# A two-layer hybrid diffusion step on one core: the queue order taken from another timing model

## The chip, the cores and the metric

The kernel runs on one core of one Trainium2 chip. The metric is device time in microseconds (us). Three runs of the kernel before took 2752.75, 2754.29 and 2756.11 us; their median, 2754.29, is the time before.

## What is computed

One inference step of a backbone with two layers (DEPTH = 2) and model width 1024. There are 128 context tokens and 1024 latent tokens, 1152 in all, everything in float32. Each layer does this:

```
h = rmsnorm(x) * (1 + scale) + shift          # shift, scale, gate from silu(cond) @ ada_w + ada_b
a_in, a_gate, f_in, f_gate, q, k, v, c_gate = split(h @ w_in)
ya = S5 diagonal state space, both directions, then gelu and a GLU with glu_w
yf = real part of a 2-D DFT over positions and channels, @ fnet_w
yc = grouped-query attention (8 heads, 2 kv heads, softmax over 1152 keys for latents)
proj = each of ya*silu(a_gate), yf*silu(f_gate), yc*silu(c_gate) @ w_branch[n]
g = sigmoid(h @ merge_w + merge_b);   x = x + gate * (sum(g * proj) @ w_out)
```

A last RMS norm follows. The outputs are both token sets, the context keys and values, and the context's final S5 states.

## The kernel before

Activations are kept transposed, channels on the 128 partitions and tokens along the free axis, in three tiles of 384 tokens. Every float32 operand of a dense product is split in two parts, a high part in the matmul format fp32r (`hh`, `whi`, made by a copy on ACT) and the remainder (`hl`, `wlo`, made by a subtraction on DVE or, for weights, on POOL). A product is then three matmuls: high by high, low by high, high by low (`mm3`, with the matmul itself in line 168).

A dense block (`dense`) is 128 output columns. For each token tile it runs 4 or 8 times three matmuls into a PSUM tile `pd`, of which there are two; then ACT or DVE evacuates it, mostly into `jo` (three slots), and SP stores `jo` to memory. `dense_ahead` loads weights into `wst` (four slots) up to three units ahead and splits them into `whi` and `wlo` (three slots each) one unit ahead.

Beside the dense blocks run the generators of the branches. `drive` and `run_some` interleave them in the program by fixed weights: the S5 setup and states (`state_gen`), the scan (`scan_gen`, 128 steps of four DVE operations each on the state tile, in the trace called `A` with the scratch tiles `ss_s`), the q, k and v part (`qkv_gen`), the S5 output matrices (`ssm_out_gen`, tiles `ss_CA`, `ss_CK`, `ss_Hg`), its result reloaded from memory (`zload_gen`, from the tensors `ydp` and `ydl`, into `jt` and `jo`), the Fourier branch (`fnet_gen`, tiles beginning `fn_`), and attention (`attn_gen`: scores in `pa`, softmax into `at_P`, transposes in `pt`, products with V in `pv`, with dense blocks between).

The context's final states are copied out by `finals`, which `scan_gen` calls behind its last step, though the column that it reads is complete after step 16:

```python
for k in range(128):
    ...                       # four DVE operations a step
    yield 800
self.finals(l)                # act(fin, H[:, :, :, 16]), transposes, a store
```

All this is only the program's order, and it is not the order in the queues. The whole program is one block of a tile framework. When the block closes, a scheduler plays the instructions through a timing model. Each time an engine can take an instruction in the model, it gets the first one in the program's order whose inputs are there and whose output has a free slot, at the model's time. So an instruction may overtake earlier ones of its engine that are not ready in the model. The sequence found this way is written into the engine's queue (DMA issues into SP's or POOL's), the slots are fixed with it, and semaphore waits are added where data cross engines. On the chip each queue runs strictly in that sequence: if the instruction at its head has to wait, all behind it wait too.

The change and the prediction touch no line of the generators. They speak of `finals` and `scan_gen` (the DVE operations are recorded at line 145, ACT's at line 142, which are helpers), of `dense` and its evacuations, of `zload_gen`, `fnet_gen` and `attn_gen`.

## Time and profile before

| what | value |
|---|---|
| median of three runs | 2754.29 us |
| profiled execution, its own time | 2752.03 us |
| its span, first to last instruction | 2750.3 us |
| mean granted PE clock | 0.985 |
| PE, PE's weight loads | 2627.0 us (96%), 2509.0 us (91%) |
| DVE, ACT, POOL | 1826.6 (66%), 1143.5 (42%), 683.4 us (25%) |
| DMA | 366.85 MB, mean 133 GB/s |

The profile is of one execution. Busy times overlap between engines. A row of the timeline has the start, the duration, the engine, the line, the operation with its output and inputs, and in brackets how long the engine was idle before it and what released it. A wait for several events is put down to the last one by the profile. The granted clock is the share of full speed that TensorE got.

### The profile page before, as it was taken

The numbers are of one execution on the slowest core, as the hardware profiler recorded it, in microseconds if no ns is written. First come the engines' busy times: TensorE is split into PE (matmuls) and PEld (weight loads), VectorE is DVE, ScalarE is ACT, GpSimd is POOL, SyncE is SP. The second block draws the span as 40 slices with busy tenths as digits, with TensorE's granted clock in tenths as the row PEclk, the third lists the DMA queues.
The fourth block names the chain that finished last, engine by engine and source line by source line (L and its number), as shares of the span: only waits on it lengthen the run. The fifth ranks groups of instructions, "written<-read, shape, count | busy, mean of one in ns | idle before, by whom it ended". The sixth has DMA issues, their size and how long they took to land. (4 is left out here: it accounts for less than half of the span.)

```text
span 2750.3 us, 44553 instructions
## 1 busy us (share of the span) xinstructions
PE 2627.0 (96%) x16092; PEld 2509.0 (91%) x16092; DVE 1826.6 (66%) x3933; ACT 1143.5 (42%) x2676; POOL 683.4 (25%) x521
## 2 busy tenths in 40 slices
PE   7998999899999999999999899999999999999998
PEld 3898999799999999999989899989989998999998
DVE  6549955856558889866572797577654788891343
ACT  5461145331355565423345322543223655553244
POOL 3241122322321020132343212233222202102223
PEclk9999999999999999999999999999999999999999
DMA  6632223566263345544543222345645334433244
GB/s 223 178 99 84 95 87 110 150 191 207 86 202 114 110 138 153 173 126 114 165 146 93 95 89 84 107 125 160 211 154 174 109 121 150 143 121 98 80 121 149
DMA packets 459997, 366.85 MB, mean 133 GB/s; under 512 B 72953, under 2 KB 432001, under 8 KB 459777
## 3 DMA queue, kind: packets, MB, share of 16 engines
q1 hardware_dynamic: 458480, 359.75, 42.9%
q0 software_dynamic: 1296, 4.26, 0.5%
q8 instruction: 127, 2.08, 0.3%
q14 instruction: 94, 0.76, 0.1%
HBM read 243.52 MB, written 120.39 MB: 132 GB/s over the span
## 5 line engine op out<-in xcount | busy, mean ns | idle before, releaser
L168 PE MATMUL pd<-hh,whi 128*128 128x384 f32 x2496 | 857.1, 344 | 24.0 <-ACT jo L142 20.1
L168 PE MATMUL pd<-hh,wlo 128*128 128x384 f32 x2496 | 844.6, 339 | 3.2 <-POOL wlo L145 3.2
L168 PE MATMUL pd<-hl,whi 128*128 128x384 f32 x2496 | 843.1, 338 | 1.3 <-DVE hl L149 1.3
L145 POOL TENSOR_TENSOR wlo<-wst,whi 128x512 fp32r<-128x512 f32 x312 | 437.9, 1405 | 1525.8 <-ACT whi L142 1404.8
L168 PEld LDWEIGHTS pd<-hh,whi 128*128 128x128 f32 x2496 | 472.5, 189 | 35.0 <-ACT jo L142 22.8
L168 PEld LDWEIGHTS pd<-hh,wlo 128*128 128x128 f32 x2496 | 472.5, 189 | 7.8 <-POOL wlo L145 5.7
L168 PEld LDWEIGHTS pd<-hl,whi 128*128 128x128 f32 x2496 | 473.1, 190 | 3.8 <-DVE hl L149 2.3
L168 PE MATMUL pd<-A,whi 128*128 128x384 f32 x1728 | 458.2, 342 | 8.2 <-ACT jo L142 4.9
L168 PEld LDWEIGHTS pd<-A,whi 128*128 128x128 f32 x1728 | 311.2, 189 | 11.7 <-ACT jo L142 5.6
L142 ACT ACTIVATE whi<-wst 128x512 fp32r<-128x512 f32 x312 | 196.0, 630 | 278.5 <-PE pd L168 190.6
L168 PE MATMUL pd<-A,wlo 128*128 128x384 f32 x864 | 293.9, 340 | 0.0
L1078 DVE TENSOR_REDUCE at_mx<-pa 128x1 f32<-128x1152 f32 x128 | 173.3, 1354 | 16.1 <-PE pa L168 15.7
L168 PE MATMUL pa<-at_K,at_Q 128*128 128x384 f32 x768 | 167.2, 347 | 8.6 <-ACT at_P L142 5.8
L142 ACT ACTIVATE at_PT<-pt 128x384 fp32r<-128x384 f32 (+1 forms) x260 | 114.9, 490 | 144.0 <-PE pt L173 143.6
L142 ACT ACTIVATE at_P<-pa,at_mx 128x1152 f32<-128x1152 f32 x128 | 158.1, 1235 | 20.7 <-DVE at_mx L1078 19.4
L168 PEld LDWEIGHTS pd<-A,wlo 128*128 128x128 f32 x864 | 163.2, 189 | 0.1
L168 PEld LDWEIGHTS pa<-at_K,at_Q 128*128 128x128 f32 x768 | 128.3, 188 | 29.0 <-ACT at_P L142 25.5
L168 PE MATMUL pt<-qkW,hh 128*128 128x384 f32 x576 | 150.7, 343 | 0.0
L168 PE MATMUL pv<-at_PT,at_V 128*128 128x256 f32 x1152 | 148.8, 283 | 0.0
L168 PEld LDWEIGHTS pv<-at_PT,at_V 128*128 128x128 f32 x1152 | 144.7, 191 | 0.8
L142 ACT ACTIVATE jo<-pd 128x384 f32<-128x384 f32 x120 | 58.0, 485 | 198.1 <-PE pd L168 96.5
L145 DVE TENSOR_TENSOR at_PT<-pt,at_PT 128x384 fp32r<-128x384 f32 (+1 forms) x260 | 133.1, 550 | 10.0 <-ACT at_PT L142 7.8
(294 smaller groups left out, 3772.3 us busy)
## 6 DMA issues: line engine op xcount, KB each, us to landing
aw<-in_ada_w_dram SPq DMA_DIRECT2D x48, 512.0 KB, 4.8
wst<-in_merge_w_dram SPq DMA_DIRECT2D x96, 256.0 KB, 3.0
wst<-in_w_in_dram SPq DMA_DIRECT2D x80, 256.0 KB, 2.9
td<-jo SPq DMA_DIRECT2D x96, 192.0 KB, 2.3
jt<-td SPq DMA_DIRECT2D x96, 192.0 KB, 2.8
wst<-in_w_out_dram SPq DMA_DIRECT2D x64, 256.0 KB, 2.9
sgd<-jo SPq DMA_DIRECT2D x72, 192.0 KB, 2.0
jt<-sgd SPq DMA_DIRECT2D x64, 192.0 KB, 2.7
```

The costliest lines, as they stand in the source:

```text
L142: return self.nc.scalar.activation(out, in_, func, **kw)
L145: return (e or self.nc.vector).tensor_tensor(out=out, in0=a, in1=b, op=op)
L168: return self.nc.tensor.matmul(out, w, x, start=first, stop=last, **kw)
L1078: nc.vector.tensor_reduce(out=mx[:, 0:1], in_=src, axis=AX.XY if m3 else AX.X, op=OP.max, negate=True)
```

## The change

One argument of the tile context is set. It selects the timing model that the scheduler plays the program through: a detailed timeline model (devices, queues and DMAs with states of their own) in place of the default, rougher one. The traced instructions, their engines and their sizes are the same; what the scheduler decides by them, the sequence in each queue, the slots and the waits that follow from these, is decided anew.

```diff
-    with tile.TileContext(nc) as tc, ExitStack() as ctx:
+    with tile.TileContext(nc, schedule_with_timeline_sim=True) as tc, ExitStack() as ctx:
         Program(ctx, tc, I, O).run()
```

## Rows read from the trace of the kernel before

**Rows 1.** The page's busy times: engine, busy us, share of the span, instructions.
```profile
PE 2627.0 (96%) x16092; PEld 2509.0 (91%) x16092; DVE 1826.6 (66%) x3933; ACT 1143.5 (42%) x2676; POOL 683.4 (25%) x521
```

**Rows 2.** Stretches: length, busy us (instructions) of each engine, clock, DMA share, GB/s.
```profile
196.00:430.00 234.00, 222.94 (x1282) 220.65 (x1281) 185.52 (x621) 69.91 (x217) 54.90 (x43) 0.97 0.31 96
482.00:607.00 125.00, 115.43 (x772) 105.96 (x771) 91.13 (x195) 41.98 (x83) 36.69 (x28) 0.97 0.57 161
798.00:1165.00 367.00, 357.48 (x2376) 340.83 (x2376) 305.89 (x515) 200.81 (x413) 57.49 (x48) 1.00 0.44 136
...
1540.00:1772.00 232.00, 220.72 (x1268) 218.10 (x1268) 182.92 (x609) 68.24 (x212) 53.23 (x43) 0.97 0.31 96
...
2140.00:2482.00 342.00, 333.37 (x2234) 317.34 (x2232) 287.82 (x484) 189.54 (x389) 54.00 (x45) 1.00 0.42 130
```

**Rows 3.** PE's waits over the span: for what, us in total, times, longest us.
```profile
PE pd L168 <- ACT jo L142: 25.1, 8, 7.8
...
PE pt L173 <- DVE at_P L1082: 8.4, 13, 1.0
PE pt L168 <- issue: 7.3, 3, 3.4
...
PE pd L168 <- POOL wlo L145: 3.2, 5, 1.5
```

**Rows 4.** Timeline of ACT in the first layer's scan.
```profile
210.78 0.63 ACT L142 ACTIVATE whi<-wst 128x512 fp32r<-128x512 f32 x1 [1.43 <-PE pd L168]
223.66 0.32 ACT L142 ACTIVATE ss_fin<-A 128x64 f32<-128x64 f32 x1 [12.25 <-DVE A L145]
223.89 0.61 ACT L142 ACTIVATE whi<-wst 128x512 fp32r<-128x512 f32 x1
224.41 0.85 ACT L142 ACTIVATE jo<-pd 128x384 f32<-128x384 f32 x2
```

**Rows 5.** Timeline of PE behind its two longest waits for `jo`.
```profile
224.93 0.69 PE L168 MATMUL pd<-hh,whi 128*128 128x384 f32 x1 [7.84 <-ACT jo L142]
...
1566.74 0.69 PE L168 MATMUL pd<-hh,whi 128*128 128x384 f32 x1 [7.83 <-ACT jo L142]
```

**Rows 6.** Stretches behind these waits, columns as in rows 2.
```profile
225.00:229.00 4.00, 4.00 (x13) 4.00 (x14) 3.79 (x14) 0.26 (x1) 0.85 (x1) 0.50 0.50 164
229.00:233.00 4.00, 4.00 (x20) 4.00 (x19) 3.72 (x17) 0.49 (x1) 0.00 (x0) 0.81 0.02 4
233.00:250.00 17.00, 17.00 (x100) 17.00 (x100) 16.11 (x54) 4.27 (x8) 4.70 (x4) 1.00 0.24 80
...
1567.00:1571.00 4.00, 4.00 (x13) 4.00 (x14) 3.79 (x15) 0.07 (x1) 0.67 (x1) 0.50 0.51 164
1571.00:1575.00 4.00, 4.00 (x22) 4.00 (x22) 3.73 (x17) 0.49 (x1) 0.00 (x0) 0.88 0.01 2
```

**Rows 7.** Timeline of DVE in the first layer's scan; the last row ends it.
```profile
200.76 1.25 DVE L145 TENSOR_TENSOR ss_s<-ss_AR,A 128x128 f32<-128x128 f32 x1
...
203.69 0.38 DVE L145 TENSOR_TENSOR ss_s<-ss_s,A 128x128 f32<-128x128 f32 x1
204.10 1.41 DVE L145 TENSOR_TENSOR A<-ss_s,ss_s 128x128 f32<-128x128 f32 x1
...
357.88 0.28 DVE L145 TENSOR_TENSOR A<-ss_s,ss_s 128x64 f32<-128x64 f32 x1
```

**Rows 8.** Timeline of POOL at the same place.
```profile
203.97 1.29 POOL L145 TENSOR_TENSOR wlo<-wst,whi 128x512 fp32r<-128x512 f32 x1 [2.20 <-ACT whi L142]
```

**Rows 9.** Timeline of ACT: two instructions that waited for a DMA.
```profile
614.32 0.52 ACT L142 ACTIVATE A<-jo 128x384 fp32r<-128x384 f32 x1 [4.32 <-DMA jo<-ydl]
...
682.64 0.21 ACT L142 ACTIVATE fn_EO<-fn_X 128x2 f32<-128x2 f32 x1 [8.67 <-DMA thb<-jo]
```

**Rows 10.** Timeline of PE behind them.
```profile
616.63 0.69 PE L168 MATMUL pd<-A,whi 128*128 128x384 f32 x1 [3.01 <-ACT jo L142]
...
683.39 0.44 PE L168 MATMUL pd<-hh,whi 128*128 128x384 f32 x1 [1.71 <-ACT jo L142]
```

## The prediction

> **What bounds the kernel now.** I read the busy times first: PE is busy 96% of the span, DVE 66% [rows 1]. So 2750.3 - 2627.0 = 123.3 us is all that PE stands idle, and nearly all that an order can give back; no instruction is taken away. Then I cut the span into stages [rows 2]. The reader is to see that the two layers give the same table twice, that the attention stages already run PE at 97.4% and 97.5%, and that the stage with the S5 output matrices has only 92.3%. Third, what PE waits for [rows 3]: one pair, a dense block's `pd` waiting for ACT to empty the last one into `jo`, holds 25.1 us in eight waits. Fourth, the timeline around the two longest of the eight.
>
> They are the clearest case of what an order can do. `ss_fin`, the copy of the prompt's final states, is written in the program behind all 128 steps of the scan. In ACT's queue it stands far ahead of that place, because its input is complete after step 16. On the chip ACT reached it at 211.4 and stood until DVE had that step, 12.25 us [rows 4]. Behind it in the same queue lay a weight split `whi` and the two `jo` copies that PE needed, so PE stood 7.84 us; in the second layer it stood 7.83 us in the same way [rows 5]. Nothing that PE needs comes from `ss_fin`.
>
> **The change, part by part.** Instructions, sizes and data flow stay; what moves is the place of each instruction in its engine's queue (SP's issues among them) and, with it, which buffer slot it takes. So every term is a wait that goes or comes.
>
> (a) `ss_fin`. What it costs today is more than the two stalls: after them PE's granted clock was 0.50 and 0.81 in two stretches of 4 us. At the full rate of 100 matmuls in 17 us, 4 us hold 23.5; there were 13 and 20, so 14 are missing, worth 14 x 0.17 = 2.4 us. The second layer had 13 and 22, worth 2.0 us [rows 6]. The price is 7.84 + 2.4 + 7.83 + 2.0 = 20.1 us. The cover is good: ACT was held 12.25 us and PE only 7.84, so 4.4 us of lateness are free, and a place that is too late costs nothing, as only an output copy follows. The term lies between 0 (the same place) and -20.1. I take -15: nearer the full end, because ss_fin need not be placed right, only some 8 us later, and the place of today shows a model in which the scan runs much too fast. What is late next? The scan itself ends at 357.9 [rows 7], while its states are first used in the stage that begins at 482; that PE comes 10 us earlier to the stage behind it leaves over 100 us, so nothing takes the gain back.
>
> [...] A step's last add took 1.41 us, from 204.10, where the operation before it took 0.38; POOL ran a 1.29 us split from 203.97. The one at 200.76 took 1.25 us [rows 7, 8]. [...]
>
> (b) The other six waits for `jo`, 25.1 - 15.7 = 9.4 us. Two are shown: ACT's queue is headed by an instruction that waits for a DMA, 4.32 us for a reload of `ydl` and 8.67 us at the input of the Fourier stage [rows 9], and PE waits behind it 3.01 and 1.71 us [rows 10]. The second layer has the like. A place behind `jo` would free them, and how late those loads land is what a rough price misses. Between 0 and -9.4 I take half, -4.7, since the loads are needed soon after and cannot move far.
>
> (c) Waits that the new order brings. No row shows them. They could be nil (no new wait). The nearest rows for the other end are those PE waits that come from a splitter or evacuation just too late: 3.2 us in 5 for `wlo`, 8.4 us in 13 for the scaled softmax [rows 3]. I take +4.7, nearer the lower of the two; the large end is the first rival. SP's order belongs here: a weight load that is issued a unit later shows as one more wait for `wlo`, 1.5 us at the longest [rows 3].
>
> (d) Start and end are left as they are: the first inputs and the last stores follow from data, not from order.
>
> The sum is -15 - 4.7 + 4.7 = -15 us. The profiled execution took 2752.0 us (its span 2750.3 and 1.7 around it), 2.3 under the median 2754.3. So 2752.0 - 15 + 2.3 = 2739 us on the scale of the median.
>
> **The rivals.**
>
> First, slower: attention loses its cover. In these stages PE mixes dense blocks of 12 matmuls between scores, transposes and PV, so that dense work fills the time a softmax takes on DVE and ACT. The greedy choice takes any ready matmul; a model in which PE's own queue fills ahead, or softmax lands later, hands out the dense blocks before the softmax needs cover, and PE then waits at the transposes. For it: DVE is 83% busy there (305.89 of 367), and each of the 128 passes hangs on it. Against it: only two `pd` buffers exist, so no more than two blocks can run ahead. Price: today the two stages idle 9.5 + 8.6 = 18.1 of 709 us; at the 7.7% of the S5 output stage they would idle 54, so +36 [rows 2]. With -15 from (a) that is 2752.0 + 36 - 15 + 2.3 = 2775 us; with no gain, 2790. It decides the sign from the point where attention idles over 15 us more, or 33 against 18.
>
> Second, slower: a new block at a queue's head of the size of `ss_fin`, one in each layer, while `ss_fin` stays or takes another bad place. Many instructions stand early in ACT's and DVE's queues on the strength of a modelled time (table copies, next-layer loads), and any could be the next. The price is that of rows 4 to 6, +20.1, less the 9.4 of (b) at best: between 2765 and 2774 us. Against it: the two layers are alike, so it takes only one wrong price, but a finer model has fewer of them.
>
> Third, no difference: the new model shares the old one's price of the scan, `ss_fin` stays, and the small waits change places. Then the time is that of today within a few us, 2749 to 2760. For it: nearly all of PE's order follows from the program's own order and the few buffers, which stay. That the option does nothing at all is part of this.
>
> **How the numbers follow.** The forecast has 0.47, the first rival 0.27, the second 0.11, no difference 0.15. What a measurement of this kernel can tell from no change is about 0.2%, 5.5 us, so faster is 0.47, same 0.15, slower 0.38. The chances lie close because the gain rests on one kind of wait, seen and priced, while the loss needs no more than a slightly wrong order where PE has least to spare. The forecast's own range runs from 2709 to 2749: its lower end is -20.1 - 9.4, less the 7.3 us of PE's waits at an issue and the 8.4 behind the softmax, -45.2 [rows 3]. The first rival without any gain ends at 2790, so the range for the time is 2709 to 2791; a total loss of attention's cover, or every middle wait gone at once, is left outside.
>
> **What would show it.** Right: `ss_fin` stands behind several more `jo` copies in ACT's order, ACT no longer waits 12 us for it, the two 7.8 us stalls and the clock of 0.50 behind them are gone, and PE's waits for `jo` fall from 25 to some 5 us. (b) right: ACT's waits for `ydl` and for the Fourier input no longer have a `jo` directly behind them. (c) right: PE's idle time in the attention stages stays near 18 us. Wrong: these stages idle over 33 us, PE waits at transposes for the softmax's scale, or ACT has a new single wait over 8 us with a `jo` behind it; and if both 7.8 us stalls are there unchanged, the step that failed is (a).

## The result, and the profile after

The changed kernel takes 2936.55 us in the median (four runs, 2931.53 to 2940.29). The kernel before, with a fourth run beside the three on which the forecast rests, takes 2753.64. The ratio is 1.0662 [1.0642, 1.0681] (the brackets hold the 95% interval): the changed kernel is slower. The forecast was 2739, the range ended at 2791, and of its rivals the first, attention losing its cover, had the right sign and place. The profiled execution took 2931.53 us with a span of 2929.7, which is 179.4 us more than before.

The busy times of the changed kernel, to be read against [rows 1]:

```profile
PE 2672.2 (91%) x16092; PEld 2551.4 (87%) x16092; DVE 1820.2 (62%) x3933; ACT 1153.9 (39%) x2676; POOL 673.5 (23%) x521
```

Each engine has the instructions that it had. PE now stands idle 2929.7 - 2672.2 = 257.5 us where it stood 123.3, and it is busy 45.2 us longer with the same 16092 matmuls; the mean granted clock is 0.969 after 0.985. So 134 us are waits. Most of the other 45 lie where the clock was lower. The clock records of the two traces hold two values, 1.0 and 0.5, and PE was busy 58.3 us at 0.5 before and 138.5 us after. Dense matmuls in a row began 0.32 us apart at 0.5 and 0.173 apart at 1.0 (the medians, the same in both traces), so 80.2 us more at 0.5 cost an estimated 80.2 x (1 - 0.173 / 0.32) = 37.

Next, where. Both spans are cut at the same landmarks, the first score matmul and the last PV product of each attention; columns as in rows 2. The kernel before:

```profile
0.00:768.10 768.10, 714.88 (x4205) 663.45 (x4206) 497.09 (x1286) 295.25 (x783) 213.84 (x165) 0.97 0.46 140
768.10:1145.00 376.90, 367.30 (x2444) 349.64 (x2443) 311.06 (x524) 203.99 (x429) 57.94 (x48) 1.00 0.44 136
1145.00:2106.20 961.20, 920.17 (x5501) 892.25 (x5500) 615.63 (x1448) 343.26 (x867) 281.32 (x204) 0.98 0.44 133
2106.20:2482.20 376.00, 367.21 (x2443) 349.82 (x2442) 311.01 (x524) 204.13 (x429) 57.86 (x48) 1.00 0.44 135
2482.20:2750.30 268.10, 257.39 (x1507) 253.88 (x1505) 91.79 (x151) 96.91 (x172) 72.43 (x56) 0.99 0.36 110
```

The same five stretches after:

```profile
0.00:809.50 809.50, 731.78 (x4252) 676.87 (x4253) 492.72 (x1289) 293.64 (x784) 214.19 (x166) 0.96 0.43 132
809.50:1247.30 437.80, 378.28 (x2418) 359.59 (x2416) 310.52 (x527) 214.69 (x433) 57.03 (x47) 0.96 0.39 123
1247.30:2226.40 979.10, 926.72 (x5526) 899.56 (x5527) 615.99 (x1445) 336.79 (x862) 273.17 (x205) 0.98 0.43 128
2226.40:2663.80 437.40, 381.38 (x2417) 362.80 (x2415) 310.95 (x527) 214.69 (x432) 57.04 (x47) 0.96 0.39 123
2663.80:2929.70 265.90, 254.01 (x1484) 252.53 (x1483) 90.06 (x145) 94.13 (x166) 72.12 (x56) 0.98 0.35 105
```

The two attention stages have 60.9 and 61.4 of the 179.4 us, the stretch ahead of the first attention 41.4, the one between the two 17.9, the end -2.2. Attention holds 26 matmuls fewer in each layer than before, so the time is not for more work: idle time rose from 9.6 + 8.8 to 59.5 + 56.0 us (97 us), busy time by 11.0 + 14.2 us.

What PE waits for (us in total, times, longest). The first wait of the changed kernel was a small one in the kernel before, and [rows 3] leave it out:

```profile
PE pa L168 <- ACT at_P L142: 5.8, 7, 1.3
```

After:

```profile
PE pa L168 <- ACT at_P L142: 64.1, 30, 2.5
PE pd L168 <- ACT jo L142: 39.2, 12, 11.1
PE pv L168 <- DVE at_PT L145: 22.3, 29, 1.2
...
PE pt L168 <- DVE qk_xn L145: 8.8, 1, 8.8
```

The first and the third line of these are softmax: a score product waits for its `pa` buffer until ACT has taken the exponential out of it, a PV product for a transposed softmax tile. The next two tables tell why. The changed kernel's attention in steps of 50 us:

```profile
1050.00:1100.00 50.00, 49.90 (x330) 49.23 (x328) 33.81 (x59) 26.48 (x54) 15.91 (x14) 1.00 0.58 178
1100.00:1150.00 50.00, 36.22 (x236) 32.52 (x235) 41.46 (x71) 25.49 (x51) 0.00 (x0) 0.97 0.17 53
1150.00:1200.00 50.00, 50.00 (x326) 49.62 (x326) 38.48 (x67) 19.91 (x39) 7.82 (x5) 1.00 0.60 184
1200.00:1250.00 50.00, 35.51 (x215) 31.44 (x214) 33.95 (x60) 25.80 (x52) 0.00 (x0) 0.90 0.17 50
```

The same stretches with the instructions of the tile `pd` alone, the dense blocks (PE, PEld, DVE, ACT, then clock, DMA share, GB/s):

```profile
1050.00:1100.00 50.00, 29.96 (x162) 27.43 (x160) 4.38 (x8) 1.75 (x3) 1.00 0.58 178
1100.00:1150.00 50.00, 4.58 (x24) 4.14 (x25) 1.55 (x3) 0.00 (x0) 0.97 0.17 53
1150.00:1200.00 50.00, 34.22 (x180) 30.79 (x180) 7.15 (x13) 0.00 (x0) 1.00 0.60 184
1200.00:1250.00 50.00, 3.19 (x17) 2.78 (x17) 0.00 (x0) 1.05 (x2) 0.90 0.17 50
```

And the same tile in the attention of before:

```profile
900.00:950.00 50.00, 22.18 (x111) 19.12 (x112) 4.96 (x9) 0.00 (x0) 1.00 0.32 98
950.00:1000.00 50.00, 20.00 (x96) 15.89 (x94) 2.75 (x5) 1.16 (x2) 1.00 0.53 165
1000.00:1050.00 50.00, 23.53 (x116) 19.68 (x116) 3.85 (x7) 0.56 (x1) 1.00 0.41 125
1050.00:1100.00 50.00, 23.10 (x116) 19.86 (x116) 5.49 (x10) 0.00 (x0) 1.00 0.52 156
```

Before, each 50 us hold 20 to 24 us of dense matmuls. After, they come in bursts: 30 us, then 5, 34, 3. In a burst PE is full, but the softmax falls behind: of ACT's instructions on the softmax's row maxima (`at_mx`) the four stretches of after hold 14, 18, 12 and 14, and each of the four before held 18. A hole is no faster than the kernel before was with its dense work beside it, so what a burst has delayed is not caught up. Between bursts POOL splits no weight, the DMA share drops from 0.60 to 0.17, and PE has little but attention itself. A piece of PE's timeline in such a hole (start, duration, what, idle time before it and its releaser):

```profile
1113.86 1.31 PE L168 MATMUL pa<-at_K,at_Q 128*128 128x384 f32 x6 [2.19 <-ACT at_P L142]
1115.01 0.49 PE L173 MATMUL pv<-ident,at_P 128*128 128x128 f32 x3
1115.34 0.82 PE L173 MATMUL pt<-ident,at_P 128*128 128x128 f32 x6
1117.09 2.40 PE L168 MATMUL pv<-at_PT,at_V 128*128 128x256 f32 x18 [0.93 <-DVE at_PT L145]
```

No dense block stands between the score, transpose and PV groups; 2.19 + 0.93 us of this pass are idle.

`ss_fin` did not go where the forecast put it. ACT, then PE, of the changed kernel around it and around a second, new block:

```profile
280.25 0.32 ACT L142 ACTIVATE ss_fin<-A 128x64 f32<-128x64 f32 x1 [10.00 <-DVE A L145]
280.48 0.85 ACT L142 ACTIVATE jo<-pd 128x384 f32<-128x384 f32 x2
...
350.11 0.31 ACT L142 ACTIVATE qk_qt<-qk_qr 128x128 fp32r<-128x128 f32 x1 [17.82 <-DVE qk_qr L145]
...
350.64 0.47 ACT L142 ACTIVATE jo<-pd 128x384 f32<-128x384 f32 x1
```

```profile
281.00 0.69 PE L168 MATMUL pd<-hh,whi 128*128 128x384 f32 x1 [2.47 <-ACT jo L142]
...
351.16 0.69 PE L168 MATMUL pd<-hh,whi 128*128 128x384 f32 x1 [11.07 <-ACT jo L142]
351.65 0.52 PE L168 MATMUL pd<-hl,whi 128*128 128x384 f32 x1
351.97 0.52 PE L168 MATMUL pd<-hh,wlo 128*128 128x384 f32 x1
...
355.72 0.34 PE L168 MATMUL pt<-qkW,hh 128*128 128x384 f32 x1
355.90 0.34 PE L168 MATMUL pt<-qkW,hl 128*128 128x384 f32 x1
```

ACT still stands 10.00 us at `ss_fin` (10.44 in the second layer), though PE loses only 2.47 us behind it here and 5.66 there. Another instruction, `qk_qt`, heads ACT's queue too early: ACT stands 17.82 us in front of it, until 350.11, with a `jo` behind it, and PE stands 11.07 us (in the second layer 12.46 and 5.71). Then PE's matmuls start 0.32 us apart, with a granted clock of 0.50 from 351 to 355, until they are 0.18 apart again at 355.72, with 1.00 from 355.7 to 360.

### The profile page after: what moved, and what is told of

Its sections match the earlier page's. It is cut to its first block, busy times and chain, and to the rows that moved or that the text cites. A ratio compares the mean times of both kernels' runs of the same rounds, so it can differ in the third digit from the quotient of the medians.

```text
span 2929.7 us, 44530 instructions
## 1 busy us (share of the span) xinstructions
PE 2672.2 (91%) x16092; PEld 2551.4 (87%) x16092; DVE 1820.2 (62%) x3933; ACT 1153.9 (39%) x2676; POOL 673.5 (23%) x521
## 5 line engine op out<-in xcount | busy, mean ns | idle before, releaser
L168 PE MATMUL pa<-at_K,at_Q 128*128 128x384 f32 x768 | 173.2, 362 | 65.5 <-ACT at_P L142 64.1
L168 PEld LDWEIGHTS pa<-at_K,at_Q 128*128 128x128 f32 x768 | 137.6, 200 | 75.1 <-ACT at_P L142 72.3
L168 PE MATMUL pv<-at_PT,at_V 128*128 128x256 f32 x1152 | 155.7, 290 | 22.5 <-DVE at_PT L145 22.3
L173 PE MATMUL pt<-ident,at_P 128*128 128x128 f32 x784 | 121.2, 283 | 2.4 <-DVE at_PT L145 2.3
```

Of the source, the lines that this page charges most:

```text
L168: return self.nc.tensor.matmul(out, w, x, start=first, stop=last, **kw)
L173: return self.nc.tensor.transpose(out, in_, i[:n, :n])
```

## The experiments

The theory under test (W where an expectation uses a letter): the detailed model has a window for each engine, a number of instructions that it may take before they can run; the changed kernel has 35 for PE and 12 for the others. These are settings of the model, and no run shows how many instructions the engines of the chip take ahead. The scheduler fixes an instruction's place when the model takes it into the window. 35 dense matmuls are 6 us of work (17 us hold 100 of them [rows 6]), so PE's places are given out some 6 us ahead, when attention's next matmul is never ready in the model and a dense one often is. The rivals: the windows of the other engines; single late instructions such as `ss_fin` and `qk_qt`; a different price of the softmax or the DMAs in the model. All times below are medians. The kernel before took 2751.07 us beside the first four kernels and 2753.3 beside the last four, and each ratio is against the one of these that belongs to it.

A count over the finished queues, not a time: of PE's matmuls and transposes the kernel before has 1309 more than 20 places off the program's order, the farthest by 82; the changed one has 8287, the farthest by 770 (outside attention; the farthest in attention is 276 off).

**PE's window cut to 2.** Kernel e1, the changed kernel with the model's window for PE set to 2 and those of the other engines left at 12.

> The changed kernel, but the number of PE instructions that the detailed model lets PE's sequencer hold ahead of the array set from 35 to 2 (the other engines' stay 12). Theory W (window): the scheduler hands an instruction out when the modelled sequencer takes it, some 6 us before it can run (35 matmuls of 0.17 us), and at that moment attention's next matmuls are never ready while dense ones are; so dense blocks run ahead in bursts and the softmax is left without cover. W expects the attention stages to fall from 437.8 and 437.4 us back to 375 to 390, and the whole to 2730 to 2800 us. Theory P (prices): the loss comes from other durations in the detailed model, of DVE, ACT and DMA, and the window has no part in it: 2900 to 2960 us, with attention stages over 425 us.

It took 2756.38 us, 1.0018 [1.0006, 1.0029] of before. One number in the model makes some 178 to 180 of the 183 us, by which of the medians of before one takes. All prices of the detailed model are still in e1, so they do not make the loss. Its stretch ahead of attention and its two attention stages:

```profile
0.00:771.00 771.00, 714.82 (x4205) 662.28 (x4206) 500.09 (x1286) 293.87 (x783) 208.59 (x165) 0.97 0.46 140
771.00:1151.00 380.00, 370.12 (x2465) 359.22 (x2463) 307.31 (x528) 212.12 (x432) 58.00 (x48) 0.99 0.44 135
2112.30:2489.90 377.60, 368.39 (x2466) 357.74 (x2464) 306.49 (x528) 212.02 (x432) 58.83 (x49) 0.99 0.44 135
```

The start is back too: 4205 matmuls and 771.0 us, as before (768.1). In the count above this kernel has 3419 places off, the farthest 132.

**The other windows cut to 2.** Kernel e2, the changed kernel with the windows for SP, ACT, DVE and POOL set to 2 and PE's left at 35.

> The changed kernel with PE's modelled window left at 35 and those of ACT, DVE, POOL and SP set from 12 to 2. Theory W in its narrow form (PE's window alone): unchanged, 2900 to 2960 us. Its wide form (every queue runs ahead too far, DVE's and ACT's above all): 2750 to 2850 us. Theory P: 2900 to 2960 us.

It took 2935.57 us, 1.0671 [1.0643, 1.07], so this changed nothing. Attention took 435.1 and 443.4 us. The windows of the other engines are out.

**PE's order held in attention alone.** Kernel e3, the changed kernel with PE's instructions kept in the program's order from attention through the gate blocks behind it:

```diff
...
+        return self.tc.keep_in_program_order(ins) if self.pin else ins
...
+            self.pin = True
...
+            self.pin = False
```

The first line goes around each matmul and transpose; the other two stand ahead of attention and behind the gate blocks.

> The changed kernel, with PE's instructions of the attention stage and of the gate blocks behind it held in the program's own order by edges that cost no wait; all else is ordered as in the change. If PE's order in these stages makes the loss (theory W), both stages fall to 375 to 395 us and the whole to 2810 to 2850 us, the rest of the loss staying at the start. If the order of DVE and ACT makes it, the stages stay over 425 us and the whole at 2900 to 2960 us.

It took 2829.78 us, 1.0281 [1.0257, 1.0306], and attention 379.9 and 380.9 us; the wait at `pa` for `at_P` fell from 64.1 to 7.7 us. So 106.8 us hang on PE's order in these stages, together with what the model makes of it on the other engines, whose places follow (ACT's queue differs from the changed kernel's in 706 places). What remains, 79 us, lies elsewhere, and half of it, 37.5 us, ahead of the first attention.

**`ss_fin` alone.** Kernel e4, the kernel before, with its own model, and one edge:

```diff
-        self.act(fin, H[:, :, :, 16])
+        self.tc.keep_in_program_order(self.act(fin, H[:, :, :, 16]))
```

> The kernel before, with one edge added: the copy of the final states (ss_fin) may not overtake what was traced ahead of it on ACT, so it no longer stands at the head of ACT's queue while the scan is at step 16. Term (a) of the prediction by itself: both waits of 7.8 us and the slow clock behind them gone, 2733 to 2740 us (-20.1 of 2753.6 at the full price). Rival: PE has no work to do earlier, and the gain is waited for again in front of the S5 output stage: 2748 to 2755 us.

It took 2729.15 us, 0.9916 [0.9895, 0.9938], less than both kernels and just under the range expected. The queues of DVE, POOL and SP are those of the kernel before, place for place; ACT's differs in 116 places and PE's in 24. Its ACT at the place, its waits for `jo`, and the scan's stretch:

```profile
349.81 0.47 ACT L142 ACTIVATE jo<-pd 128x384 f32<-128x384 f32 x1
350.17 0.31 ACT L142 ACTIVATE ss_fin<-A 128x64 f32<-128x64 f32 x1
```

```profile
PE pd L168 <- ACT jo L142: 9.1, 5, 2.9
```

```profile
196.00:430.00 234.00, 230.98 (x1343) 228.92 (x1342) 191.32 (x627) 74.27 (x240) 56.69 (x44) 0.99 0.32 99
```

No wait stands before `ss_fin`; the waits for `jo` fell by 16.0 us, and the same 234 us hold 61 matmuls more than in [rows 2] at a clock of 0.99 after 0.97. The gain, 21.9 us (17 to 29 by the interval), agrees with the price of the two stalls and the slow clock behind them, 20.1.

**All of PE in the program's order.** Kernel e5, the changed kernel with `pin = True` throughout.

> The changed kernel with every PE instruction of the program held in the program's own order; the other engines are ordered by the detailed model with its windows as in the change. Theory W (PE's order by the modelled window makes the whole loss, the rest that stayed in e3 too): 2740 to 2790 us. Rival: what stayed in e3, 79 us, comes from the order of the other engines or of the DMAs: 2800 to 2830 us.

It took 2907.88 us, 1.0557 [1.0541, 1.0572]. Both theories missed. Attention is as short as in e3 (377.4 and 381.1 us), but strict order costs more elsewhere. Its PE waits:

```profile
PE pt L168 <- DVE fn_G L145: 40.8, 15, 6.3
...
PE pa L173 <- ACT qk_qo L142: 19.4, 8, 3.9
```

PE has to overtake in the Fourier stage and in the q and k part; the program's order there is not one to run. The run therefore says nothing of e3's remaining 79 us.

**PE's window at 8.** Kernel e6, as e1 with PE's window set to 8.

> As e1, with PE's modelled window at 8 in place of 2 (the change has 35). Theory W: the loss grows with the distance that is run ahead, so between e1 and the change, 2765 to 2860 us, with attention stages of 382 to 415 us. If the loss only depended on running ahead at all, it would be at 2900 us or more; if 8 is still short against the 12 matmuls of a dense group, near e1, under 2765 us.

It took 2772.05 us, 1.0077 [1.0057, 1.0098], and attention 392.5 and 390.6 us; it has 4552 places off, the farthest 204. With 2, 8 and 35 the time is 2756, 2772 and 2937 us: it rises with the window. The wait at `pa` for `at_P`, 64.1 us at 35, is here

```profile
PE pa L168 <- ACT at_P L142: 13.4, 9, 2.1
```

**Window 2 and the late `ss_fin`.** Kernel e7, the edits of e1 and e4 together.

> e1 with the edge of e4 (ss_fin not ahead of what was traced before it on ACT). In e1 the two waits at ss_fin are shorter than in the kernel before, 4.5 us at the longest on PE, so the gain should be half of e4's, 8 to 14 us: 2742 to 2748 us. If the detailed model with a short window is better in other places, this is under e4's 2729 us; theory W does not say so.

It took 2746.88 us, 0.9975 [0.9965, 0.9986], 9.5 under e1. It is still 17.7 us over e4 (15.5 when each is set against its own kernel before). PE's waits for `jo` on ACT are down to 4.5 us in 6, and others are longer than in e4: 11.8 us for `jo` on DVE after 3.2, and 11.3 for `fn_G` after 6.3.

**Dense work early under the old model.** Kernel e8, the kernel before with 30 steps of the dense generator run ahead of the attention that they were to cover:

```diff
             m = merges()
+            self.run_some(m, 30)
```

> The kernel before, with its default model, where 30 of the steps of dense work (12 matmuls each, 62 us of PE at full rate) that the program spreads over the attention stage are traced ahead of that stage in each layer. It makes by hand what theory W says that the changed order does. W: the last passes of attention run without cover, each bare step some 1 to 1.5 us longer, so 30 to 45 us a layer, with idle PE at the softmax: 2800 to 2850 us. Rival (dense work ahead of attention is harmless, and the loss of the change came from something else in its order): 2745 to 2765 us.

It took 2923.81 us, 1.0624 [1.0602, 1.0646]. The direction is as expected; the loss is 170.5 us where some 47 to 97 were expected. Its main wait, then the dense blocks' instructions in two stretches of its attention:

```profile
PE pa L168 <- ACT at_P L142: 100.9, 55, 2.3
```

```profile
1100.00:1150.00 50.00, 0.00 (x0) 0.00 (x0) 0.00 (x0) 0.00 (x0) 0.90 0.09 27
1150.00:1200.00 50.00, 0.00 (x0) 0.00 (x0) 0.00 (x0) 0.00 (x0) 0.86 0.06 15
```

The rough model, with its old rules, gives a loss of the changed kernel's size and the same kind of wait when dense work is merely done too soon. But e8 puts 360 dense matmuls a layer ahead of attention, and the changed kernel's attention has only 26 fewer than before: there most of the dense work stays in the stage and comes unevenly. So e8 shows what a lack of cover costs, not the way in which the change came to it. Attention is longer than before, 392.0 and 401.1 us, although some 62 us of dense work have left each. And `ss_fin` is where it was: the loss needs no new block at a queue's head.

**What is shown and what is open.** It is shown that PE's window in the model makes the loss (e1, e2, e6), that the greater part is PE's order in attention (e3), and that attention without its dense work makes such a loss by itself (e8). It is not shown why the dense work comes in bursts with pauses and not in one early run. Nor is one window of 35 the whole run-ahead: up to 144 dense matmuls stand in the queue ahead of attention work that the program has before them (in the kernel before at most 27), so it adds up over many choices, and how it does was not followed. In a pause POOL splits nothing, so the weights' loads or splits stop too; which comes first was not tried. The 41 us ahead of the first attention were not taken apart further than that window 2 gives them back; three single waits there, 11.07 behind `qk_qt`, 8.81 for `qk_xn` and 5.63 for the loads `aw`, add up to 25.5 us.

## Why the prediction was wrong

**The step that failed** is the bound set against the first rival: "only two `pd` buffers exist, so no more than two blocks can run ahead". A `pd` buffer holds a block only until it is evacuated into `jo`, and each evacuation frees it for the next block. In the program nothing ties the sequence of dense blocks to that of the softmax passes, so two buffers bound how many blocks are open at a time, not how far the work is ahead. The finished queues show it. One can count the dense matmuls that stand ahead of one of attention's matmuls though the program has them behind it. In the kernel before there are at most 27 at any place, out of no more than two fills of `pd`, so the bound described the old order. In the changed kernel there are up to 144, out of up to 11 fills; with window 2 (e1) up to 53, out of four. With attention alone held in order (e3) there are none, and PE's instructions more than 20 places off fall from 8287 to 3817. This bound was the only argument against the rival, which got 0.27 and a small price; its mechanism, "a model in which PE's own queue fills ahead", is what the runs found.

**The rival's price.** It was +36 us, from the idle share of another stage (7.7%). Measured, attention has 13.6% and 12.8% idle and costs 122 us: 97 idle and 25 of longer busy time. That is mostly the clock, which the price left out although [rows 6] had shown 0.50 behind two waits: in the two stages PE was busy 59.8 us at 0.5, and not at all before; at 0.32 against 0.173 us a matmul that is an estimated 27 us. The range left out "a total loss of attention's cover". The stage was a poor proxy: attention's dense blocks are its only cover, and e8 shows what it has without them, 34 us of PE in 50.

**(a) `ss_fin`, -15.** The price is right, but this change does not bring it. The 20.1 us came out as 21.9 in e4. But the detailed model shares the old one's error: ACT stood there 10.00 and 10.44 us. "I take -15: nearer the full end, because ss_fin need not be placed right" took it that the new model prices the scan better; a finer model was taken for a more exact one without a row that says so. That PE lost 2.47 and 5.66 us behind it, not 7.84 and 7.83, is no more than half of the term. That scan operations were longer beside POOL's splits is shown by more than the two in [rows 7]: of the 1024 scan operations of the kernel before (both layers), the 47 that began during a split of POOL all took over 0.8 us (1.36 in the median), and the other 977 took 0.28 in the median, five of them over 0.8. What makes them longer was not shown. And it is less than half of the wait at `ss_fin`. Up to the step that `ss_fin` needs, three operations began so in the first layer before, some 1.1 us longer each than 0.28, where ACT stood 12.25, and four after, where it stood 10.00. What the models have wrong about the scan is not shown.

**(b) the other `jo` waits, -4.7.** This term failed too, by its own test: the instructions that wait for a DMA still have a `jo` directly behind them. Here is the changed kernel's ACT at the input of the Fourier stage, then PE behind it and behind the reload of `ydl`, against [rows 9] and [rows 10]:

```profile
721.63 0.21 ACT L142 ACTIVATE fn_EO<-fn_X 128x2 f32<-128x2 f32 x1 [8.93 <-DMA fn_X<-fd]
721.74 0.58 ACT L142 ACTIVATE jo<-pd,hmb 128x384 f32<-128x384 f32 x1
```

```profile
649.83 1.01 PE L168 MATMUL pd<-A,whi 128*128 128x384 f32 x2 [2.86 <-ACT jo L142]
...
722.37 0.44 PE L168 MATMUL pd<-hh,whi 128*128 128x384 f32 x1 [1.96 <-ACT jo L142]
```

With their like in the second layer these waits were 8.3 us before and are 9.1 after. In e7 the waits for `jo` on ACT are 4.5 us, 4.6 under e4's 9.1, but those for `jo` on DVE are 8.6 longer, so no run shows the gain.

**(c) new waits, +4.7.** This was too small even with little run-ahead. e7 has the gain of (a), as e4 has, and the rest of the detailed order leaves it 15.5 to 17.7 us over e4. "No row shows them" was true, and the upper row taken, 8.4 us, was no bound.

**(d) start and end "left as they are".** The end is (-2.2 us), the start is not: 41.4 us more ahead of attention, or 33 when the 47 matmuls that moved there are taken off at 0.17 us. A new block at a queue's head, the second rival, is part of it: `qk_qt`, 11.07 us on PE here and 5.71 in the second layer. So two rivals came true together, and the text had priced them one at a time.

Of the three signs of being wrong that it named, two came: "these stages idle over 33 us", with 115 us, and "a new single wait over 8 us with a `jo` behind it", with the 17.82 us in front of `qk_qt`. The third, PE waiting at the transposes for the softmax's scale, did not: PE waits at the scores, for their buffer `pa`.

## What to carry to other kernels

Work that covers another stage's latency is worth something only at its time. Before you say that buffers hold it back, ask who frees the buffer: if the same stream of work frees it itself, nothing holds it, and a scheduler that gives out places ahead of time will spend it early. And when one wait in a queue has been seen and priced, mend that instruction alone: here one line gave 0.9916 [0.9895, 0.9938], where a new order for everything gave 1.0662 [1.0642, 1.0681].

## What was not expected of the hardware

The clock also fell without any long wait, where PE stood only a little at a time: in e8's attention, where no single wait in the two stretches above and between 2500 and 2600 us is over 2.3 us, the granted clock was 0.90 and 0.86 in the first two and 0.83 in the third, with 70.3 us of 100 busy. The changed kernel's two attention stages show the same: but for one wait near the start of each, 4.7 and 3.5 us for `jo` on DVE, no wait there is over 2.5 us, and the clock is 0.96 in each, where it was 1.00 before. There 0.96 is a mean: the clock record has 0.5 for 30.7 and 37.5 us of the two stages, 6.8 us of each next to that wait, and 1.0 for the rest.
